# Feed-forward entries of a two-layer model: gate multiplied into the sigmoid ahead, high parts written by ScalarE from the transposes, a first group of five tiles

## The chip, the core and the metric

The kernel runs on one core of a Trainium2 chip. The metric is the device time of one launch in microseconds (us), lower is better. On the core TensorE (PE in the profile) multiplies matrices, VectorE (DVE), ScalarE (ACT) and GpSimd (POOL) work on tiles, and SyncE (SP) issues most transfers. PSUM, where TensorE writes its results, is used as 8 banks of 128 rows by 512 float32 columns. Everything is float32 at the kernel's edges.

## What is computed

A model of two layers, 512 rows of 1024 features. Each layer has a mixer and a feed-forward, each behind an RMS norm that is modulated by a condition vector, and each added to x through a gate vector:

```python
for i in range(DEPTH):                       # DEPTH = 2
    sh_m, sc_m, g_m, sh_f, sc_f, g_f = split(silu(c) @ ada_w[i] + ada_b[i], 6)
    h = rms_norm(x, norm_mix[i]) * (1.0 + sc_m) + sh_m
    y = dsa_attention(h, ...) if i % 2 == 0 else s5_mixer(h, ...)
    x = x + g_m * y
    h = rms_norm(x, norm_ffn[i]) * (1.0 + sc_f) + sh_f
    x = x + g_f * conv_ffn(h, ...)           # up 1024 -> 5632, conv, silu(gate)*val, down to 1024
# the end of s5_mixer:  ga, gb = split(gelu(y) @ w_glu);  return ga * sigmoid(gb)
```

## The kernel before, in words

x lies in SBUF as four blocks of 128 rows (b0 to b3). A float32 product is made of three products of numbers that are split into a high and a low part: high by high, high by low, low by high (`mm3`). So each operand is split once: a high part, rounded to the format `fp32r`, and a low part, the operand minus its high part. Weights arrive by SP's transfers as `raw` tiles; ScalarE casts them to `wh`, VectorE subtracts to `wl`.

All work is written as Python tasks that yield their operations. A planner (`Sched`) picks the next operation by its own costs and writes the instructions of each engine in that order, so the order of a queue is fixed when the kernel is built, and an engine never overtakes. Every operation is recorded at line 310. Where the planner sees a gap of more than 1.6 us ahead on TensorE, it fills it with products whose result nobody uses (`warm`, line 759). Operations that may run on either of two engines (`Alt`) are placed by the planner.

Both feed-forwards are entered through `norm_block` (line 798), once per block of rows. For block b: `norm_rows` squares the rows on ScalarE (`jk`, with the sum in `ss`), VectorE makes `rs_v`, GpSimd raises it to the power -1/2 (`rs_r`), VectorE scales the rows to `xn`. Then for each half of the features (hf 0 and 1, called b1h0 and so on below) TensorE transposes four squares of 128 into one PSUM bank (`nt`), ScalarE applies the modulation to the four (`ht`, in SBUF), VectorE casts the 512 columns to the high part of `H` and subtracts to its low part.

The up-projection in `ffn` (line 1197 on) has 44 weight tiles of 128 columns per layer. A tile is 24 products of 512 columns (8 features blocks by 3). The first group of tiles is made in two parts: part 0 multiplies the columns of blocks b0 and b1 (24 products of 256 columns for each tile), part 1 those of b2 and b3. Part 0 can so begin when `H` of b0 and b1 is written. A tile of the group occupies one PSUM bank from part 0 to the end of part 1.

The feed-forward of layer 1 (FFN1 below) follows the GLU of the mixer: `b_post` takes the sigmoid of the gb products (`sg`), `a_post` multiplies by the ga products (VectorE, `sg<-acc,sg`), by the gate vector (GpSimd, `sg<-sg,gate`), and adds to x (VectorE). These last products (`acc`) end block by block, b0 to b3, 24 products apart; each block then goes to `norm_block`. The feed-forward of layer 0 (FFN0) follows the output projection of the attention in the same way.

Of the kernel before, what the change touches and what calls it, by code (L numbers as in the profile page):

```python
# [14 lines left out]
AF = mybir.ActivationFunctionType  # L15
ALU = mybir.AluOpType
# [3 lines left out]
P = 128  # L20
# [3 lines left out]
KT = 8  # L24
# [147 lines left out]
class Sched:  # L172
# [13 lines left out]
    def spawn(self, gen, prio):  # L186
        t = Task()
        self.n += 1
        t.gen, t.prio, t.ops, t.cond, t.n, t.ready, t.name, t.alts = gen, prio, None, None, self.n, 0.0, gen.__name__, ()
        self.tasks.append(t)  # L190
        self.advance(t)
# [211 lines left out]
def tile_kernel(ctx: ExitStack, tc, t, out):  # L403
    nc = tc.nc
    Z = Sched()
    V, S, G, PE, SP = (Engine(k, e) for k, e in (
        ("V", nc.vector), ("S", nc.scalar), ("G", nc.gpsimd), ("PE", nc.tensor), ("SP", nc.sync)))
# [15 lines left out]
    tmp = Res(Z, tpool, "tmp", TMPS, 512)  # L423
    bank = Res(Z, psum, "bank", 8, 512)
    state = {"side": 0, "side_max": 3, "units": 0, "done": 0}
    flags = set()
    spawn = Z.spawn
# [4 lines left out]
    def need(banks=0, tmps=0, quads=0):  # L432
        return lambda: (state["side"] + banks <= state["side_max"] and bank.free() >= banks
                        and tmp.free() >= tmps and quad.free() >= quads)

    def sbank(name):
        state["side"] += 1
        return bank.get(name)

    def sput(*b):  # L440
        state["side"] -= len(b)
        bank.put(*b)
# [18 lines left out]
    acol = const.tile([P, 4, KT], F32)  # L461
# [93 lines left out]
    gates = {}  # L555
# [242 lines left out]
    def norm_block(b, ni, sh, H, key):  # L798
        xn = yield from norm_rows(b)
        for hf in range(2):  # L800
            yield need(banks=1, tmps=1)
            pt = sbank("nt")
            ht = tmp.get("ht", [P, 4, P])
            yield [PE.transpose(pt[:, j * P:(j + 1) * P], xn[:, (4 * hf + j) * P:(4 * hf + j + 1) * P], ident)
                   for j in range(4)]
            bs = slice(b * P, (b + 1) * P)
            for j in range(4):
                k = 4 * hf + j
                yield S.activation(ht[:, j], pt[:, j * P:(j + 1) * P], AF.Identity, scale=acol[:, ni, k:k + 1],
                                   bias=sh[:, k:k + 1])  # L810
            sput(pt)
            ks = slice(4 * hf, 4 * hf + 4)
            yield V.tensor_copy(H[:, ks, 0, bs], ht)
            yield V.tensor_sub(H[:, ks, 1, bs], ht, H[:, ks, 0, bs])
            tmp.put(ht)
            flags.add((key, hf, b))
        quad.put(xn)
        flags.add((key, b))
# [351 lines left out]
    def ffn(layer, Hs, then, last, hready, mid=None):  # L1170
        yield has("conv")
        A = {}
        vals = {}

        def up_post(m, ps):
            yield need(tmps=1)
            cv = tmp.get("cv")
            w = cw[:, layer, m]
            yield S.activation(cv, ps, AF.Identity, scale=w[:, 2:3], bias=cb[:, layer, m:m + 1])
            yield V.scalar_tensor_tensor(cv[:, 1:], ps[:, :L - 1], w[:, 1:2], cv[:, 1:], op0=ALU.mult, op1=ALU.add)  # L1180
            yield V.scalar_tensor_tensor(cv[:, 2:], ps[:, :L - 2], w[:, 0:1], cv[:, 2:], op0=ALU.mult, op1=ALU.add)
            bank.put(ps)
            if m % 2 == 0:
                vals[m // 2] = cv
                return
            yield S.activation(cv, cv, AF.Silu)
            yield lambda: m // 2 in vals
            yield V.tensor_mul(cv, cv, vals[m // 2])
            tmp.put(vals[m // 2])
            yield lambda: quad.free() >= 1  # L1190
            a = quad.get("a", [P, 2, L], F32R)
            yield S.copy(a[:, 0], cv)
            yield V.tensor_sub(a[:, 1], cv, a[:, 0])
            tmp.put(cv)
            A[m // 2] = a

        def up(m, group, parts):

            ws_ = []
            ps = [None] * group  # L1200
            n = L // parts
            for pt in range(parts):
                for g in range(group):
                    yield lambda: hready((pt + 1) * n)
                    if pt == 0:
                        ws_.append((yield from WS.get()))
                        yield lambda: bank.free() > 0
                        ps[g] = bank.get("up")
                    else:
                        WS.hold = WS.stop = len(plan) if layer else glu0  # L1210
                    wh, wl = ws_[g]
                    o = ps[g][:, pt * n:(pt + 1) * n]
                    for k in range(KT):
                        ws = slice(k * P, (k + 1) * P)
                        h0, h1 = Hs[:, k, 0, pt * n:(pt + 1) * n], Hs[:, k, 1, pt * n:(pt + 1) * n]
                        yield [PE.matmul(o, wh[:, ws], h0, start=(k == 0), stop=False),
                               PE.matmul(o, wh[:, ws], h1, start=False, stop=False),
                               PE.matmul(o, wl[:, ws], h0, start=False, stop=(k == KT - 1))]
                    if pt == parts - 1:
                        quad.put(wh, wl)  # L1220
                        spawn(up_post(m + g, ps[g]), 2)

        for half in range(2):
            i = 0
            while i < 2 * HT:
                g = 4 if half == 0 and i == 0 else 1
                yield from up(2 * HT * half + i, g, 2 if g > 1 else 1)
                i += g
                flags.add(("up", layer, half))
            if half == 1 and mid:  # L1230
                mid()
            k0 = half * HT
            lh = lambda k, b: A[k0 + k][:, 0, b * P:(b + 1) * P]
            ll = lambda k, b: A[k0 + k][:, 1, b * P:(b + 1) * P]
            for ch in range(2):
                fin = then if half and ch else None
                if last and half == 1:
                    def fin(b, ch=ch):
                        yield DM(out[0, b * P:(b + 1) * P, ch * 512:(ch + 1) * 512], x[:, b, ch * 512:(ch + 1) * 512])
                tl = 7 if half and ch and not last else 3  # L1240
                yield from gemm(HT, 512, lh, ll, resid(layer, 5, ch, fin, half and not ch and not last, pre_ssm), tail=tl,
                                ready=lambda k: k0 + k in A,
                                mid=(lambda: quad.put(*[A[k0 + k] for k in range(HT - tl)])) if ch else None)
            quad.put(*[A[k0 + k] for k in range(HT - tl, HT)])
# [578 lines left out]

    sg = {}

    def b_post(b, ps):
        yield need(tmps=1)
        sg[b] = tmp.get("sg")
        yield S.activation(sg[b], ps, AF.Sigmoid)
        bank.put(ps)  # L1830

    def a_post(ch, then):
        def post(b, ps):
            yield lambda: b in sg and (1, 2) in gates
            s_ = sg.pop(b)
            yield V.tensor_mul(s_, ps, s_)
            bank.put(ps)
            yield G.tensor_mul(s_, s_, gates[1, 2][:, ch * 512:(ch + 1) * 512])
            xs = x[:, b, ch * 512:(ch + 1) * 512]
            yield V.tensor_add(xs, xs, s_)  # L1840
            tmp.put(s_)
            if ch:
                yield from then(b)
            else:
                yield from first_half(b)
        return post


    def main():
        yield has("consts")  # L1850
        H = new_H()
# [81 lines left out]
        for b0 in (0, 2):  # L1933
            acc = {}
            for k in range(KT):
                yield lambda: ("g", k // 2) in flags
                if k // 2 == len(tiles):
                    tiles.append((yield from WS.get()))
                w, s_ = tiles[k // 2], k % 2 * 512
                for b in (b0, b0 + 1):  # L1940
                    if b not in acc:
                        yield lambda: bank.free() > 0
                        acc[b] = bank.get("acc")
                    yield mm3(acc[b], gh[0](k, b), gh[1](k, b), w[0][:, s_:s_ + 512], w[1][:, s_:s_ + 512], k == 0, k == KT - 1)
                    if k == KT - 1:
                        spawn(b_post(b, acc[b]), 2)
            state["side_max"] = 4
        quad.put(*[v for w in tiles for v in w])
        state["side_max"] = 3
        yield from gemm(KT, 512, gh[0], gh[1], a_post(0, None), tail=4)  # L1950
        yield from gemm(KT, 512, gh[0], gh[1], b_post, tail=4)
        H1 = new_H()
        yield from gemm(KT, 512, gh[0], gh[1], a_post(1, to_ffn(1, H1)), tail=8)
        quad.put(*[v for q in range(4) for v in HG[q]], gates[1, 2])
# [113 lines left out]
```

## Time and profile before

| what | value |
|---|---|
| median of 3 runs (lowest, highest) | 1284.19 us (1284.01, 1284.42) |
| the profiled execution: its own time | 1281.76 us |
| its span in the trace | 1280.0 us |
| TensorE busy | 1256.0 us, 98% of the span |
| mean granted TensorE clock | 0.997 |
| VectorE, ScalarE, GpSimd busy | 845.5, 519.0, 321.0 us |

The span is the time from the first to the last instruction of the profiled execution; 1.76 us of its own time lie outside of it. That execution is 2.43 us shorter than the median of the runs.

### The profile page before, as it was taken

What the parts mean: (1) busy time and instruction counts of PE and PEld (TensorE: products, weight loads), DVE (VectorE), ACT (ScalarE), POOL (GpSimd) and SP (SyncE); (2) the same over time, 40 slices, a digit from 0 to 9 for tenths busy, and PEclk for the clock granted to TensorE, in tenths of its full rate; (3) what the DMA queues carried; (4) which work ended last, traced back from release to release, by engine and by line L of the source; (5) the groups of instructions that cost most, each with busy time, mean ns of one, the idle gap of its engine ahead of it and who ended that gap; (6) DMA issues with size and microseconds to landing.
All of it is one profiled execution on the core that took longest, in us unless ns stands there. A gap on an engine that the chain in (4) does not pass through costs nothing. (4 is left out here: it accounts for less than half of the span.)

```text
span 1280.0 us, 19538 instructions
## 1 busy us (share of the span) xinstructions
PE 1256.0 (98%) x7314; PEld 993.3 (78%) x7314; DVE 845.5 (66%) x1600; ACT 519.0 (41%) x1124; POOL 321.0 (25%) x525
## 2 busy tenths in 40 slices
PE   7999999999999999999999999999999999999998
PEld 6766577666877678888888887788987888888887
DVE  6688697788677777768775468633787643666632
ACT  4345555556544344234443222423544432244420
POOL 0234446832144256343310302211200001000010
PEclk9999999999999999999999999999999999999999
DMA  9948522101377763445444289322443323322221
GB/s 375 367 161 315 180 82 72 45 34 67 130 291 244 241 234 115 144 173 153 147 127 171 91 183 404 138 100 81 165 133 139 99 91 124 109 76 80 80 88 62
DMA packets 76471, 195.59 MB, mean 153 GB/s; under 512 B 15053, under 2 KB 25805, under 8 KB 76377
## 3 DMA queue, kind: packets, MB, share of 16 engines
q1 hardware_dynamic: 72808, 191.43, 43.4%
q10 hardware_dynamic: 3568, 2.92, 0.8%
q8 instruction: 57, 0.93, 0.3%
q14 instruction: 38, 0.30, 0.1%
HBM read 172.01 MB, written 20.21 MB: 150 GB/s over the span
## 5 line engine op out<-in xcount | busy, mean ns | idle before, releaser
L310 PE MATMUL up<-H,wh 128*128 128x512 f32 (+1 forms) x1536 | 444.7, 374 | 0.0
L310 PEld LDWEIGHTS up<-H,wh 128*128 128x128 f32 x1536 | 277.8, 188 | 61.6 <-issue 12.1
L310 PE MATMUL up<-H,wl 128*128 128x512 f32 (+1 forms) x768 | 285.5, 372 | 0.0
L310 DVE TENSOR_TENSOR wl<-raw,wh 128x1024 fp32r<-128x1024 f32 (+1 forms) x192 | 234.8, 1230 | 61.4 <-ACT wh L310 52.8
L310 PE MATMUL acc<-wh,H 128*128 128x512 f32 (+3 forms) x752 | 241.5, 388 | 1.5 <-ACT H L310 1.4
L310 ACT CAST wh<-raw 128x1024 fp32r<-128x1024 f32 (+1 forms) x192 | 192.5, 1015 | 106.8 <-DMA raw<-in_w_down_dram 41.8
L310 PE MATMUL acc<-wh,a 128*128 128x512 f32 x704 | 219.0, 390 | 0.0
L310 DVE SCALAR_TENSOR_TENSOR cv<-up,sm_b,cv 128x511 f32<-128x511 f32 (+1 forms) x176 | 131.6, 748 | 90.0 <-ACT cv L310 87.0
L310 PEld LDWEIGHTS acc<-wh,H 128*128 128x128 f32 x752 | 138.8, 188 | 46.6 <-issue 20.2
L310 PEld LDWEIGHTS up<-H,wl 128*128 128x128 f32 x768 | 144.6, 188 | 25.3
L310 PEld LDWEIGHTS acc<-wh,a 128*128 128x128 f32 x704 | 132.2, 188 | 27.6 <-issue 0.4
L310 ACT ACTIVATE cv<-up,sm_b 128x512 f32<-128x512 f32 x88 | 68.6, 780 | 197.9 <-PE up L310 180.7
L310 PE MATMUL acc<-wl,H 128*128 128x512 f32 (+3 forms) x376 | 141.4, 376 | 0.0
L310 PE MATMUL acc<-wl,a 128*128 128x512 f32 x352 | 137.0, 389 | 0.0
L310 POOL TENSOR_TENSOR x<-x,rt 128x512 f32<-128x512 f32 x20 | 31.5, 1578 | 416.0 <-DVE rt L310 407.9
L310 DVE TENSOR_TENSOR rt<-acc,gate 128x512 f32<-128x512 f32 x40 | 27.5, 689 | 101.0 <-PE acc L310 101.0
L310 PEld LDWEIGHTS acc<-wl,H 128*128 128x128 f32 x376 | 70.8, 188 | 9.9
L310 PEld LDWEIGHTS acc<-wl,a 128*128 128x128 f32 x352 | 66.1, 188 | 13.6
L310 POOL TENSOR_TENSOR rs_r<-rs_v,nhalf 128x1 f32<-128x1 f32 (+1 forms) x32 | 36.5, 1145 | 99.5 <-DVE rs_v L310 99.4
L310 ACT ACTIVATE cv<-cv 128x512 f32<-128x512 f32 x44 | 27.8, 632 | 68.5 <-DVE cv L310 66.5
L310 POOL TENSOR_TENSOR rm<-rm,rn 128x256 f32<-128x256 f32 (+3 forms) x46 | 37.2, 838 | 62.7 <-DVE rn L310 54.9
L310 PE MATMUL ada<-raw,cond_r 128*32 128x512 f32 (+1 forms) x544 | 49.3, 451 | 2.7 <-ACT xT L310 1.4
(268 smaller groups left out, 1517.4 us busy)
## 6 DMA issues: line engine op xcount, KB each, us to landing
raw<-in_ada_w_dram SPq DMA_DIRECT2D x96, 512.0 KB, 6.4
raw<-in_w_up_dram SPq DMA_DIRECT2D x88, 512.0 KB, 4.1
raw<-in_w_down_dram SPq DMA_DIRECT2D x40, 512.0 KB, 3.5
raw<-in_w_qkv_dram SPq DMA_DIRECT2D x24, 512.0 KB, 6.5
raw<-in_w_glu_dram SPq DMA_DIRECT2D x16, 512.0 KB, 9.3
k_d<-zq SPq DMA_DIRECT2D x8, 512.0 KB, 6.1
raw<-in_w_out_dram SPq DMA_DIRECT2D x8, 512.0 KB, 3.9
p_d<-p SPq DMA_DIRECT2D x16, 256.0 KB, 2.4
```

The lines of the kernel that those rows point to most:

```text
L310: op.fn(*op.a, **op.k)
```

## The change

Four edits. In `norm_block` ScalarE now writes the high part of `H` straight from the transposes in PSUM, and VectorE makes `ht` from the same transposes; the cast of `ht` on VectorE is gone. The first group of up tiles has five tiles in place of four. The gate vector is multiplied into the sigmoid `sg` ahead, on GpSimd or VectorE, and no longer behind the ga products. `b_post` takes the half of the features as an argument for that.

```diff
 # norm_block
             for j in range(4):
                 k = 4 * hf + j
-                yield S.activation(ht[:, j], pt[:, j * P:(j + 1) * P], AF.Identity, scale=acol[:, ni, k:k + 1],
+                yield S.activation(H[:, k, 0, bs], pt[:, j * P:(j + 1) * P], AF.Identity, scale=acol[:, ni, k:k + 1],
                                    bias=sh[:, k:k + 1])
+                yield V.tensor_scalar(ht[:, j], pt[:, j * P:(j + 1) * P], acol[:, ni, k:k + 1], sh[:, k:k + 1],
+                                      op0=ALU.mult, op1=ALU.add)
             sput(pt)
             ks = slice(4 * hf, 4 * hf + 4)
-            yield V.tensor_copy(H[:, ks, 0, bs], ht)
             yield V.tensor_sub(H[:, ks, 1, bs], ht, H[:, ks, 0, bs])
 # ffn
-                g = 4 if half == 0 and i == 0 else 1
+                g = 5 if half == 0 and i == 0 else 1
 # the GLU
-    def b_post(b, ps):
-        yield need(tmps=1)
-        sg[b] = tmp.get("sg")
-        yield S.activation(sg[b], ps, AF.Sigmoid)
-        bank.put(ps)
+    def b_post(ch):
+        def post(b, ps):
+            yield need(tmps=1)
+            s_ = tmp.get("sg")
+            yield S.activation(s_, ps, AF.Sigmoid)
+            bank.put(ps)
+
+            yield lambda: (1, 2) in gates
+            yield Alt(*[E.tensor_mul(s_, s_, gates[1, 2][:, ch * 512:(ch + 1) * 512]) for E in (G, V)])
+            sg[b] = s_
+        return post
     def a_post(ch, then):
         def post(b, ps):
-            yield lambda: b in sg and (1, 2) in gates
+            yield lambda: b in sg
             s_ = sg.pop(b)
             yield V.tensor_mul(s_, ps, s_)
             bank.put(ps)
-            yield G.tensor_mul(s_, s_, gates[1, 2][:, ch * 512:(ch + 1) * 512])
             xs = x[:, b, ch * 512:(ch + 1) * 512]
             yield V.tensor_add(xs, xs, s_)
```

How the instructions stand on three engines at the entry of FFN1 follows; a name before `<-` is what is written, those behind it are read, and `waits` lists the engines or queues whose semaphores the instruction waits for. Of the eight gate multiplies three stand on VectorE now and five on GpSimd, all ahead of the ga products.

ScalarE, at the end of the GLU, before: the squares of b0 (first row), then the two halves of b0 with the squares of b1 between them.

```order
L310 ACTIVATE jk,ss<-x 128x512 [waits DVE_49]
L310 ACTIVATE ht<-nt,mods,acol 128x128 [waits PE_49,Activation_49]
L310 ACTIVATE ht<-nt,mods,acol 128x128 x3
L310 ACTIVATE jk,ss<-x 128x512 [waits DVE_49]
L310 ACTIVATE ht<-nt,mods,acol 128x128 [waits PE_49,Activation_49]
L310 ACTIVATE ht<-nt,mods,acol 128x128 x3
```

The same place of ScalarE with the change:

```order
L310 ACTIVATE jk,ss<-x 128x512 [waits DVE_49]
L310 ACTIVATE H<-nt,mods,acol 128x128 [waits PE_49]
L310 ACTIVATE H<-nt,mods,acol 128x128 [waits DVE_49] x3
L310 ACTIVATE jk,ss<-x 128x512
L310 ACTIVATE H<-nt,mods,acol 128x128 [waits PE_49]
L310 ACTIVATE H<-nt,mods,acol 128x128 [waits DVE_49] x3
```

Before, the second to fourth activation of a half waited for nothing; now each of them waits for VectorE.

VectorE at the same place, before: the ga product and x of b0, `xn` of b0, x of b1, the two halves of b0 with `rs_v` and `xn` of b1 between them.

```order
L310 TENSOR_TENSOR sg<-acc,sg 128x512 [waits PE_49]
L310 TENSOR_SCALAR xn<-x,rs_r 128x1024 [waits Pool_49]
L310 TENSOR_TENSOR x<-x,sg 128x512 [waits Pool_49]
L310 CAST H<-ht 128x4x128 [waits Activation_49]
L310 TENSOR_TENSOR H<-ht,H 128x4x128 [waits DVE_49]
L310 TENSOR_SCALAR rs_v<-ss,e_9136 128x1 [waits Activation_49]
L310 TENSOR_SCALAR xn<-x,rs_r 128x1024 [waits Pool_49]
```

VectorE with the change, from `xn` of b0 to the low part of b0's second half:

```order
L310 TENSOR_SCALAR xn<-x,rs_r 128x1024 [waits Pool_49]
L310 TENSOR_TENSOR sg<-acc,sg 128x512 [waits PE_49]
L310 TENSOR_SCALAR ht<-nt,acol,mods 128x128 [waits Activation_49]
L310 TENSOR_TENSOR x<-x,sg 128x512 [waits DVE_49]
L310 TENSOR_SCALAR ht<-nt,acol,mods 128x128 [waits Activation_49] x3
L310 TENSOR_TENSOR H<-ht,H 128x4x128 [waits DVE_49]
L310 TENSOR_SCALAR rs_v<-ss,e_9166 128x1 [waits Activation_49]
L310 TENSOR_SCALAR ht<-nt,acol,mods 128x128 [waits Activation_49] x2
L310 TENSOR_SCALAR xn<-x,rs_r 128x1024 [waits Pool_49]
L310 TENSOR_SCALAR ht<-nt,acol,mods 128x128 [waits Activation_49] x2
L310 TENSOR_TENSOR H<-ht,H 128x4x128 [waits DVE_49]
```

Four `ht` instructions stand where one cast stood, each of them waits for ScalarE, and `xn` of b1 stands between the second and the third `ht` of b0's second half.

TensorE, the last rows of the GLU and the first of the up-projection, before:

```order
L310 MATMUL acc<-wl,H 128x512
L310 MATMUL acc<-wh,H 128x512
L310 MATMUL nt<-sm_a,xn 128x128 x4
L759 MATMUL warm<-sm_a 128x128 x17
L310 MATMUL up<-H,wh 128x256 x2
L310 MATMUL up<-H,wl 128x256
```

TensorE with the change:

```order
L310 MATMUL acc<-wl,H 128x512
L310 MATMUL acc<-wh,H 128x512
L310 MATMUL nt<-sm_a,xn 128x128 x4
L310 MATMUL acc<-wh,H 128x512
L310 MATMUL acc<-wl,H 128x512
L310 MATMUL acc<-wh,H 128x512
L310 MATMUL up<-H,wh 128x256 x2
L310 MATMUL up<-H,wl 128x256
```

The `warm` products are gone, and the transposes have moved: in the change those of b0h0, b0h1, b1h0, b1h1 and b2h0 stand 48, 36, 27, 15 and 3 products ahead of the up-projection (before, b0h0 to b1h1 stood 39, 27, 18 and 0 products ahead of it), and b2h1, b3h0 and b3h1 stand behind 42, 69 and 99 of the 120 products of part 0 (before, b2's and b3's four stood behind 30, 39, 51 and 63 of 96). At the entry of FFN0 five `warm` and at that of FFN1 seventeen are gone, for which the trace has ten and 34 records; the other `warm` of the program stay. There too b2h0 now stands three products ahead of the up-projection, and b2h1 and b3h0 48 and 69 products into part 0.

## Rows read from the trace of the kernel before

**Rows 1.** The page, parts 1 (busy us, share, instructions) and 2 (granted clock).

```profile
PE 1256.0 (98%) x7314; PEld 993.3 (78%) x7314; DVE 845.5 (66%) x1600; ACT 519.0 (41%) x1124; POOL 321.0 (25%) x525
PEclk9999999999999999999999999999999999999999
```

**Rows 2.** The chain that ended last, from FFN1's entry: start us, us, what.

```profile
907.98 0.44 PE nt L310 x4
908.42 3.80 PE warm L759 x34
912.22 3.59 PE up L310 x30
...
921.50 42.70 PE up L310 x249
...
1036.14 59.84 PE acc L310 x264
```

**Rows 3.** Timeline, FFN1's entry: start us, us, engine, operation, [idle before, releaser].

```profile
890.26 0.69 DVE L310 TENSOR_TENSOR sg<-acc,sg 128x512 f32<-128x512 f32 x1 [1.51 <-PE acc L310]
...
891.10 1.28 POOL L310 TENSOR_TENSOR sg<-sg,gate 128x512 f32<-128x512 f32 x1 [25.53 <-DVE sg L310]
...
892.41 0.69 DVE L310 TENSOR_TENSOR x<-x,sg 128x512 f32<-128x512 f32 x1 [1.46 <-POOL sg L310]
...
893.14 0.63 ACT L310 ACTIVATE jk<-x 128x512 bf16<-128x512 f32 x1 [5.84 <-DVE x L310]
...
894.19 0.55 POOL L310 TENSOR_TENSOR rs_r<-rs_v,nhalf 128x1 f32<-128x1 f32 x1 [1.81 <-DVE rs_v L310]
...
896.31 0.74 DVE L310 TENSOR_SCALAR xn<-x,rs_r 128x1024 f32<-128x1024 f32 x1
...
897.55 0.60 PE L310 MATMUL nt<-sm_a,xn 128*128 128x128 f32 x4
...
898.25 1.50 ACT L310 ACTIVATE ht<-nt,mods,acol 128x128 f32<-128x128 f32 x4 [4.38 <-PE nt L310]
...
900.25 0.69 DVE L310 TENSOR_TENSOR H<-ht,H 128x512 fp32r<-128x512 f32 x1
```

**Rows 4.** The tile `ht`: min, median and max ns of its instructions.

```profile
L310 ACT ACTIVATE ht<-nt,mods,acol x64: 447/457/464, 335.5 to 923.6; 128x128 f32<-128x128 f32 x64
```

**Rows 5.** VectorE's groups by form: busy us, mean ns, idle before (`pt` is in PSUM).

```profile
L310 DVE COPY pT<-pt 128x128 f32<-128x128 f32 x9 | 2.5, 285 | 1.5 <-PE pt L310 1.3
...
L310 DVE TENSOR_SCALAR ct<-c_in 128x128 f32<-128x128 f32 x4 | 1.4, 348 | 0.0
...
L310 DVE TENSOR_SCALAR c_in<-c_in 128x128 f32<-128x128 f32 x4 | 0.9, 220 | 0.0
```

**Rows 6.** Timeline, two engines that read one PSUM bank (`pv`).

```profile
764.19 0.42 DVE L310 COPY U<-pv 128x256 f32<-128x256 f32 x1 [0.98 <-PE pv L310]
764.64 0.37 ACT L310 COPY U<-pv 128x256 f32<-128x256 f32 x1 [1.89 <-DVE U L310]
```

**Rows 7.** Timeline, the split of one weight tile.

```profile
908.63 1.22 DVE L310 TENSOR_TENSOR wl<-raw,wh 128x1024 fp32r<-128x1024 f32 x1
...
909.90 1.05 ACT L310 CAST wh<-raw 128x1024 fp32r<-128x1024 f32 x1
```

**Rows 8.** Timeline of TensorE, FFN0's entry.

```profile
340.60 0.60 PE L310 MATMUL nt<-sm_a,xn 128*128 128x128 f32 x4
...
348.14 0.40 PE L310 MATMUL up<-H,wh 128*128 128x256 f32 x2
...
363.31 1.28 PE L759 MATMUL warm<-sm_a 128*128 128x128 f32 x10
```

**Rows 9.** Windows: length, busy us (instructions) of each engine, granted clock, DMA share, GB/s.

```profile
0.00:16.00 16.00, 10.22 (x112) 8.41 (x113) 8.53 (x33) 8.31 (x18) 2.71 (x8) 1.00 0.90 346
750.00:762.00 12.00, 9.46 (x84) 9.16 (x82) 5.81 (x13) 3.27 (x10) 0.80 (x5) 1.00 1.04 192
762.00:770.00 8.00, 8.00 (x96) 7.82 (x96) 4.89 (x12) 2.03 (x3) 0.00 (x0) 0.57 1.04 404
```

More of the change, by code (lines that the diff above doesn't have):

```diff
@@ L1945, in main @@
                     if k == KT - 1:
-                        spawn(b_post(b, acc[b]), 2)
+                        spawn(b_post(0)(b, acc[b]), 2)
             state["side_max"] = 4
@@ L1950, in main @@
         yield from gemm(KT, 512, gh[0], gh[1], a_post(0, None), tail=4)
-        yield from gemm(KT, 512, gh[0], gh[1], b_post, tail=4)
+        yield from gemm(KT, 512, gh[0], gh[1], b_post(1), tail=4)
         H1 = new_H()
```

## The prediction

> **What bounds the kernel now.** I read the page first: TensorE is busy 98% of the span at a granted clock of nine tenths or more in every slice [rows 1]. So a change pays only through what TensorE executes, or through time in which it waits. The chain of waits says the same at the places that the change touches: from FFN1's entry on every piece is TensorE's, piece behind piece. Two prices come from it. A product of 512 columns costs 59.84 / 264 = 0.227 us, one of 256 columns 3.59 / 30 = 0.12 us, and four transposes 0.44 us [rows 2]. And there is one piece that does no work: 3.80 us of `warm`, between the last transposes and the first up product. There TensorE has nothing to do until `H` of b1 is written. FFN0's entry has a smaller such piece, 1.28 us, within part 0 [rows 8]. Behind 921.50 the 249 up products (129 of 256 columns and 120 of 512, 15.5 + 27.2 = 42.7 us) run without a wait [rows 2]. So before, each entry costs TensorE only its `warm`: what feeds it is just fast enough.
>
> The timeline shows how that feeding runs, for one block. From the end of x of b0 to `rs_r` it takes 892.41 + 0.69 to 894.19, so 1.1 us, and `rs_r` and `xn` take 0.55 and 0.74. For one half, the first transpose starts at 897.55, the four activations at 898.25 (0.70 later) and last 1.50, and the low part ends at 900.94: 2.7 us from the first activation to the end of `H` [rows 3]. Neither ScalarE nor VectorE holds the other up within the four squares.
>
> **What the change removes and adds on TensorE.** Gone are the two `warm` pieces, 3.80 + 1.28 = 5.1 us. A fifth tile in two parts is 48 products of 0.12 in place of 24 of 0.227: 0.32 us more in each layer, 0.64 in all [rows 2]. If all else stays hidden, that is a gain of 4.4 us. [...]
>
> **The gate edit.** Behind the ga product GpSimd's multiply goes, 1.28 us here with its hops from 890.95 to 892.41 = 1.46 us, so x of a block is complete 1.4 us sooner [rows 3]. The eight multiplies ahead stand where VectorE and ScalarE wait for products; I cost them at nothing, for TensorE works on the GLU meanwhile and nothing reads `sg` until the ga products end. Were that cover gone it would be a VectorE row of 0.69 for each of three.
>
> **The price of a pair.** This is the step that decides. ScalarE's write to `H` and VectorE's `ht` read one bank, and each now waits for the other: the four squares go ScalarE, VectorE, ScalarE, VectorE. The trace shows that a second reader of a bank starts only behind the first: 764.19 + 0.42, then 764.64, a hop of 0.03 us [rows 6]. An activation of a square is 0.457 us [rows 4]. `ht` on VectorE from PSUM is not in the trace. The nearest row in size and source is the copy of a 128x128 square from PSUM, 0.285; the nearest in operation, both in SBUF, are 0.220 and 0.348 [rows 5]. I take 0.285, for its source is the same, and keep the other two as bounds. A pair is then 0.457 + 0.03 + 0.285 + 0.04 = 0.81 us (0.745 to 0.875), four of them 3.2, and with the low part 0.69 a half takes 3.9 us where it took 2.7. [...]
>
> Worse than the 1.2 us: both queues are in order, so whatever stands between two `ht` (x, `xn`, the 1.22 us subtraction of a weight tile, [rows 7]) now stops ScalarE too, and ScalarE's squares and its 1.05 us casts stop VectorE. For one block eight pairs take 6.5 us, two low parts 1.4, and `xn`, the ga product and x 2.1, some of it beside an activation: about 9 us. TensorE gives one block every 24 x 0.227 + 2 x 0.44 = 6.3 us. So it will wait, more with each block.
>
> **FFN1, followed through the new order** (times on the axis of before; order from the three engines' rows). The acc products end at 907.98; without three interleaved transposes of 0.44 and with b0h0's 48 products ahead of their end, those transposes start at 895.8, and the first activation at 896.5 or so. Pair 1 ends at 897.4; VectorE then adds x of b1 (to 898.1), so pair 2 ends at 898.4, pairs 3 and 4 at 899.2 and 900.0, the low part at 900.7. The squares of b1 stand behind the fourth activation on ScalarE and end at 900.5, `rs_r` at 901.5. The first pairs of b0h1 run from 900.5 to 902.1, and only then `xn` of b1, to 902.9. TensorE reaches b1h0's transposes at 901.4: **1.5 us of wait**. The rest of b0h1 ends at 904.7, b1h0 with the ga product and x of b2 in between at 908.9, the squares of b2 at 909.1, three pairs of b1h1 at 911.5, `xn` of b2 at 912.3. TensorE is at b2h0's transposes at 909.1: **3.2 us**. Three products later the up-projection starts, about 913.4, where it started at 912.22 behind its `warm`. In part 0 b2's pairs share VectorE and ScalarE with two or three weight tiles (1.22 and 1.05 each), x of b3 ends at 919.6, its squares stand behind a cast and end at 920.4, `xn` of b3 at 924.3. TensorE comes to b3h0 69 products (8.3 us) and one set of transposes into part 0, 922.0: **2.3 us**. Part 1 starts at 931.3 and wants b3h1 after 12 products, at 932.7; that half's four pairs and two weight subtractions end at 934.2: **1.5 us**. Together 8.5 us.
>
> **FFN0 likewise.** b1h0's transposes stand where they stood, 340.60, and `xn` of b1 comes behind six pairs, the squares and a low part at 341.8: **1.2 us**. b2h0's come 24 products later, at 348.1 with that wait, `xn` of b2 at 351.2: **3.0**, so the up-projection starts about 352.4, not 348.14 [rows 8]. b3h0: two weight casts and subtractions and two chunks of transfers on ScalarE's queue stand among b2's pairs; `xn` of b3 at 365.1, TensorE there at 362.1: **3.0**. Its last half ends about when part 1 asks. Together 7.2 us.
>
> **Sum.** -5.1 + 0.64 + 8.5 + 7.2 = +11.3 us on the 1281.76 us of the profiled execution: 1293.0. The runs' median lies 2.43 above it: **1295.4 us**. Pairs at 0.745 or 0.875 instead of 0.81, about 26 in each layer on this path: 3.4 us less or more, 1292.0 to 1298.8.
>
> **Rivals.**
> *Half the waits.* My chain goes by medians and lets no activation start before its transposes are all done; if the waits are half as long (7.9 us), the time is 1287.6; at a third, 1285.0. For it: VectorE's other work fits partly beside activations. Against: the strict alternation leaves little beside.
> *The change does what it says (the other side).* The pairs stay ahead of TensorE, because x comes 1.4 us sooner and b0's transposes stand nine products earlier, and `warm` is replaced by work: -4.4 us, 1279.8. It decides at a block of 6.3 us on VectorE and ScalarE: then no lead is lost. Against: the eight pairs alone take 6.5. Break-even is at waits of 4.4 us in all.
> [...]
>
> **Numbers.** 0.2% of the time, 2.6 us, is about what a measurement of this kernel can tell from no change. Forecast, 1291 to 1299: 0.58. Clock or dearer pairs, above that: 0.12. A third to half of the waits: 0.18, of which 0.07 within 0.2% of before. Hidden: 0.12, of which 0.08 faster and 0.04 within. So faster 0.08, same 0.11, slower 0.81. The range runs from 1285 to 1300: it leaves out the hidden case and the dearest part of the clock's.
>
> **What would show it.** In the trace after: `ht` from `nt` on VectorE at about 0.285 us, activations of squares 0.8 us apart where they were 0.35; no `warm` at the two entries; TensorE waiting for `xn` at b1h0, b2h0 and b3h0, most at b2h0; the up-projection of FFN1 starting about as late as before in spite of 3.8 us less `warm`; a granted clock as before. I am wrong if activations and `ht` overlap, if TensorE's waits at the entries stay under 5 us in all, or if something outside of the two entries moves by more than 1 us.

## Result: 1297.6 us, 1.2% slower

The changed kernel took 1297.59 us (median of 4 runs, 1295.40 to 1298.89) against 1284.10 before (4 runs, 1283.67 to 1284.42). The ratio is 1.0116, 95% interval 1.0102 to 1.0130. The profiled execution took 1298.14 us with a span of 1296.4.

The page's parts 1 and 2 of the changed kernel, against [rows 1]:

```profile
PE 1261.0 (97%) x7318; PEld 997.2 (77%) x7318; DVE 862.6 (67%) x1631; ACT 525.0 (40%) x1124; POOL 326.7 (25%) x542
PEclk9999999999999999999999989999899999999999
```

TensorE is busy 5 us longer in a span that is 16.4 us longer: most of the loss is idle time. Its waits by what they waited for (total us, times, longest), the two largest of the rows that the kernel before does not have:

```profile
PE nt L310 <- DVE xn L310: 10.9, 6, 3.2
...
PE up L310 <- DVE H L310: 1.9, 1, 1.9
```

Their places in the timeline of TensorE, FFN0 first (the bracket is the idle time before the row):

```profile
343.69 0.63 PE L310 MATMUL nt<-sm_a,xn 128*128 128x128 f32 x4 [1.36 <-DVE xn L310]
...
353.40 0.66 PE L310 MATMUL nt<-sm_a,xn 128*128 128x128 f32 x4 [3.13 <-DVE xn L310]
...
367.45 0.66 PE L310 MATMUL nt<-sm_a,xn 128*128 128x128 f32 x4 [1.31 <-DVE xn L310]
...
911.87 0.66 PE L310 MATMUL nt<-sm_a,xn 128*128 128x128 f32 x4 [1.27 <-DVE xn L310]
...
921.66 1.11 PE L310 MATMUL nt<-sm_a,xn 128*128 128x128 f32 x4 [3.19 <-DVE xn L310]
...
935.01 0.66 PE L310 MATMUL nt<-sm_a,xn 128*128 128x128 f32 x4 [0.66 <-DVE xn L310]
...
945.70 0.38 PE L310 MATMUL up<-H,wh 128*128 128x256 f32 x1 [1.94 <-DVE H L310]
```

In each entry these are the transposes of b1h0, b2h0 and b3h0, in that order; the last row is part 1 of FFN1, which waits for the low part of b3h1. Together 12.9 us. The `warm` of [rows 2] and [rows 8] is gone.

The chain that ended last, from FFN1's entry on (start us, us, what), is no longer TensorE's alone:

```profile
904.85 0.45 PE nt L310 x4
905.32 0.47 ACT H L310
905.82 0.41 DVE ht L310
906.23 0.60 DVE x L310
906.83 0.35 DVE ht L310
907.20 0.47 ACT H L310
907.69 0.42 DVE ht L310
...
921.66 1.11 PE nt L310 x4
922.78 1.28 PE acc L310 x3
924.06 6.62 PE up L310 x42
...
1052.52 59.84 PE acc L310 x264
```

For 17 us it runs through the pairs: ScalarE, VectorE, ScalarE, VectorE, with x of the next block between two of them. The up-projection starts at 924.06, 11.8 us later than in [rows 2]; the down-projection at 1052.52, 16.4 later. The price of a pair stands in the timeline of the two engines:

```profile
906.14 0.68 DVE L310 TENSOR_TENSOR x<-x,sg 128x512 f32<-128x512 f32 x1
906.26 0.46 ACT L310 ACTIVATE H<-nt,mods,acol 128x128 fp32r<-128x128 f32 x1 [0.48 <-DVE ht L310]
906.75 0.41 DVE L310 TENSOR_SCALAR ht<-nt,acol,mods 128x128 f32<-128x128 f32 x1
907.20 0.46 ACT L310 ACTIVATE H<-nt,mods,acol 128x128 fp32r<-128x128 f32 x1 [0.48 <-DVE ht L310]
```

From one activation to the next 0.94 us (906.26 to 907.20), of which ScalarE idles 0.48. Before, four activations took 1.50 in one piece [rows 3]. `ht` takes 0.41 us. The tile `ht` (min, median and max ns; then idle time of its engine before it, and who waited for it) sums it up:

```profile
L310 DVE TENSOR_SCALAR ht<-nt,acol,mods x64: 398/410/413, 337.6 to 944.5; 128x128 f32<-128x128 f32 x64
...
  ACT H L310: 18.8, 39
...
  ACT H L310: 28.8, 43
```

VectorE idled 18.8 us for ScalarE's `H` (39 times), and ScalarE 28.8 us for VectorE's `ht` (43 times).

And one thing beside the waits: the windows around b2h0's waits (length, busy us, then the granted clock third from the right):

```profile
354.00:358.00 4.00, 4.00 (x20) 3.77 (x19) 3.07 (x9) 1.01 (x3) 2.80 (x11) 0.57 0.23 58
...
922.00:928.00 6.00, 6.00 (x29) 5.71 (x27) 3.51 (x6) 2.68 (x5) 0.00 (x0) 0.54 0.31 115
928.00:932.00 4.00, 4.00 (x36) 4.00 (x35) 4.00 (x7) 2.97 (x6) 0.00 (x0) 1.00 0.41 116
```

Behind each of the two waits of 3.1 and 3.2 us TensorE worked for some microseconds at about half of its clock: 0.57 and 0.54 on the mean of these windows, 0.50 in each single microsecond from 355 to 357 and from 922 to 927 us, and 1.00 from 358 to 366 and from 928 to 935 us. By the windows' clocks, 0.43 x 4 + 0.46 x 6 = 4.5 us of full speed were lost there (an estimate; how much of it the kernel's time shows is taken up below). [rows 9] show such a stretch in the kernel before, 8 us at 0.57.

### The profile page after: what moved, and what is told of

It is laid out like the page before. It is cut to its first block, busy times and chain, and to the rows that moved or that the text cites. A ratio compares the mean times of both kernels' runs of the same rounds, so it can differ in the third digit from the quotient of the medians.

```text
span 1296.4 us, 19552 instructions
## 1 busy us (share of the span) xinstructions
PE 1261.0 (97%) x7318; PEld 997.2 (77%) x7318; DVE 862.6 (67%) x1631; ACT 525.0 (40%) x1124; POOL 326.7 (25%) x542
## 5 line engine op out<-in xcount | busy, mean ns | idle before, releaser
L310 PE MATMUL up<-H,wh 128*128 128x512 f32 (+1 forms) x1568 | 449.5, 372 | 1.9 <-DVE H L310 1.9
L310 PEld LDWEIGHTS up<-H,wh 128*128 128x128 f32 x1568 | 284.1, 190 | 62.6 <-issue 12.1
L310 PE MATMUL up<-H,wl 128*128 128x512 f32 (+1 forms) x784 | 289.4, 369 | 0.0
L310 PEld LDWEIGHTS up<-H,wl 128*128 128x128 f32 x784 | 149.1, 190 | 24.9
L310 POOL TENSOR_TENSOR C<-u,u 128x144 f32<-128x144 f32 x48 | 33.4, 711 | 104.3 <-DVE u L310 74.9
```

The source lines that it names most:

```text
L310: op.fn(*op.a, **op.k)
```

## The experiments

The theory: ScalarE and VectorE read one bank in strict alternation, a half takes too long, and TensorE waits for `xn` and `H`. The rivals: the five tiles (banks held, products split), the gate edit (work moved to VectorE), VectorE's greater work in itself, and the lower clock rather than the waits. Medians of different groups of runs come from different chips (the kernel before took 1283.12, 1281.94 and 1284.66 us on the three of this section), so the ratio to the kernel before, run on the same chip, is what counts.

**Undo the norm block.** The changed kernel with `norm_block` of before:

```diff
-                yield S.activation(H[:, k, 0, bs], pt[:, j * P:(j + 1) * P], ...)
-                yield V.tensor_scalar(ht[:, j], pt[:, j * P:(j + 1) * P], ...)
+                yield S.activation(ht[:, j], pt[:, j * P:(j + 1) * P], ...)
+            yield V.tensor_copy(H[:, ks, 0, bs], ht)
```

> The changed kernel with the norm block of before (four activations to ht, one cast, one subtraction); the gate ahead and the five tiles stay. If the alternation of ScalarE and VectorE on one bank is the cause, the waits for xn at the two entries (10.9 us in the changed kernel), the 1.9 us wait for the low part and the stretches at the lower clock go, and what is left is the sum without waits, -5.1 + 0.64: 1279 to 1282 us. If the five tiles or the gate edit are the cause, it stays at 1293 us or more.

Measured 1277.50 us against 1283.12, ratio 0.9953 (0.9939 to 0.9968): not only no loss, but faster than before, and below the expected band. The chain at FFN1's entry:

```profile
908.90 0.44 PE nt L310 x4
909.34 1.39 PE acc L310 x6
910.73 4.68 PE up L310 x39
...
922.46 37.65 PE up L310 x238
```

It is TensorE's alone again, with no `warm` and no wait: the gate edit and the five tiles do what the sum without waits said. The whole loss goes with the norm block's edit.

**Each edit alone on the kernel before.** First the norm block, as in the change's diff:

> The kernel before with the new norm block alone. If the alternation is the cause: 1294 to 1302 us, with waits for xn of 10 us or more in all. If it needs the other edits beside it: within 3 us of before.

1305.64 us, ratio 1.0168 (1.0151 to 1.0185), above the expected band: worse than the whole change. Its waits by what they waited for:

```profile
PE nt L310 <- DVE xn L310: 10.7, 5, 3.1
...
PE up L310 <- DVE H L310: 4.4, 4, 2.2
```

15.1 us, and beside them `warm` products that the planner put where TensorE then had a wait as well, in FFN1's part 0:

```profile
941.17 4.47 PE L759 MATMUL warm<-sm_a 128*128 128x128 f32 x24
...
945.91 1.50 PE L759 MATMUL warm<-sm_a 128*128 128x128 f32 x12
```

The gate edit alone:

> The kernel before with the gate edit alone. Its order has no warm at FFN1's entry any more, so if the feeding keeps up it gains that, 1280 to 1282 us. If the gate edit's work on VectorE and GpSimd is what holds TensorE up, 1287 us or more.

1279.96 us, ratio 0.9970 (0.9960 to 0.9979), at the lower edge of what was expected: it takes the `warm` at FFN1's entry away, since x of a block is complete sooner and the transposes move ahead.

The five tiles alone (`g = 5`):

> The kernel before with the five tiles alone. Its order loses the warm at FFN0's entry (1.28 us) and keeps that at FFN1's; the split costs 0.64: 1283 to 1285 us. If five banks held by the first group starve the side work: 1287 us or more.

1284.21 us, ratio 1.0000 (0.9988 to 1.0011), as expected: no change that the runs can tell, and no harm. The two rivals among the edits fall.

**The same instructions without the alternation.** First, one handover of the bank for a half in place of seven:

```diff
             for j in range(4):
                 yield S.activation(H[:, k, 0, bs], pt[:, j * P:(j + 1) * P], ...)
+            for j in range(4):
                 yield V.tensor_scalar(ht[:, j], pt[:, j * P:(j + 1) * P], ...)
```

> The changed kernel with all four activations of a half ahead of the four VectorE instructions: one handover of the bank in a half in place of seven, the same instructions otherwise. If the alternation is the cause: ScalarE is free after 1.5 us, a half takes about 1.5 + 4 x 0.41 + 0.69 = 3.8 us with VectorE 2.3 us busy, so a block takes VectorE about 6.7 us against 6.3 of TensorE: waits of 2 to 8 us in all, 1280 to 1288 us. If VectorE's 0.41 us for each square is the cause by itself: 1293 us or more.

1281.63 us, ratio 0.9989 (0.9978 to 1.0001). A half in its timeline:

```profile
902.97 1.50 ACT L310 ACTIVATE H<-nt,mods,acol 128x128 fp32r<-128x128 f32 x4 [1.07 <-PE nt L310]
904.88 1.36 DVE L310 TENSOR_SCALAR ht<-nt,acol,mods 128x128 f32<-128x128 f32 x4
...
906.27 0.69 DVE L310 TENSOR_TENSOR H<-ht,H 128x512 fp32r<-128x512 f32 x1
```

Four activations take 1.50 us again, so 0.35 from one to the next, and four `ht` behind one another 1.36, so 0.32. In a row each instruction thus overlaps its neighbour by about 0.1 us (0.46 and 0.41 us long, 0.35 and 0.32 apart), which the alternation gives up, together with a hop of 0.03 to 0.04 at each change of engine. A half takes 3.6 us from its first activation to the end of its low part for b0h0 (899.79 to 903.42), where the first one of the changed kernel takes 4.45 (905.32 to 909.77). And the engines no longer stop each other: over the whole program VectorE idles 2.1 us for `H` in place of 18.8, and ScalarE never for `ht`. This reordering alone takes the ratio from 1.0116 to 0.9989.

Second, two banks for a half, two squares in each; ScalarE begins with one bank, VectorE with the other:

```diff
-            pt = sbank("nt")
+            pts = [sbank("nt"), sbank("nt2")]
+            sq = lambda j: pts[j // 2][:, (j % 2) * P:(j % 2 + 1) * P]
...
+                i = (j + 2) % 4
-                yield V.tensor_scalar(ht[:, j], pt[:, j * P:(j + 1) * P], ...)
+                yield V.tensor_scalar(ht[:, i], sq(i), ...)
```

> The changed kernel with the transposes of a half in two banks, two squares in each: ScalarE begins with one, VectorE with the other, and they change once. The same eight instructions for a half. If the shared bank is the cause: a half takes about 2 x 0.41 + 0.05 + 2 x 0.41 + 0.69 = 2.4 us, nearly all waits go, 1277 to 1282 us. If the count or the price of VectorE's instructions is the cause: 1290 us or more.

1281.40 us, ratio 0.9995 (0.9986 to 1.0004). Its timeline at FFN1's entry:

```profile
897.52 0.81 ACT L310 ACTIVATE H<-nt,mods,acol 128x128 fp32r<-128x128 f32 x2 [3.49 <-PE nt L310]
897.91 1.05 DVE L310 TENSOR_SCALAR ht<-nt,acol,mods 128x128 f32<-128x128 f32 x3
898.67 0.81 ACT L310 ACTIVATE H<-nt,mods,acol 128x128 fp32r<-128x128 f32 x2 [0.34 <-DVE ht L310]
```

The two engines read transposes at once, from two banks: ScalarE from 897.52 to 898.33, VectorE from 897.91 on. The instructions are the changed kernel's, eight for a half, so neither their number nor VectorE's greater work is the cause: taking turns on one bank, square by square, is. A bank that is handed over once does little harm, as the run ahead of this one shows (1.0 us of waits for `xn`, where the changed kernel has 10.9). The planner laid both versions anew, but their transposes of b0h0 to b2h0 stand about where the changed kernel's do: 48, 36, 27, 12 and 3 products ahead of FFN1's up-projection with one handover, 48, 39, 30 and 18 ahead and 3 behind its start with two banks. So it is not that TensorE asks for its blocks later. No run here lets the two engines read one bank at once (in the changed kernel each of a half's instructions behind its first waits for the other engine), so what that would do to the time is not shown.

**The clock.** Twelve products without use ahead of b2's first transposes, at both entries:

```diff
+            if b == 2 and hf == 0:
+                yield [PE.matmul(pt[:, :P], ident, ident, start=True, stop=True) for _ in range(12)]
             yield [PE.transpose(...) for j in range(4)]
```

> The changed kernel with twelve products without use on TensorE ahead of the transposes of b2's first half, at both entries: they lie in the time in which TensorE waits 3.1 us for xn, 24 records or about 2.7 us. If the lower clock behind those waits is a cost of its own (6 us at 0.50 and 3 us at 0.53 to 0.62 in the changed kernel, so about 4.5 us in all): 1292 to 1294 us and a granted clock of 1.00 at the entries. If the waits alone make the time: 1297 us or a little more.

1294.12 us, ratio 1.0102 (1.0086 to 1.0117). The kernel before took 1281.94 on this chip, so the band in microseconds says little, and by the ratio the gain on 1.0116 lies within the intervals. Windows of it:

```profile
922.00:928.00 6.00, 5.63 (x48) 5.43 (x47) 5.35 (x10) 3.97 (x7) 1.46 (x1) 1.00 0.47 155
936.00:940.00 4.00, 1.32 (x12) 1.12 (x10) 2.91 (x6) 1.38 (x3) 0.00 (x0) 1.00 0.39 117
940.00:944.00 4.00, 3.82 (x19) 3.82 (x20) 0.44 (x2) 0.78 (x1) 0.00 (x0) 0.57 0.08 29
```

The clock stays at 1.00 behind b2h0's transposes, but a wait of 2.9 us later on, for a low part, now has the stretch at 0.57 behind it. Nor is the fill free: its products take 2.84 us at each entry and a wait of 1.14 and 1.17 is left, at each place 0.8 more than the wait alone was. So I ran it beside the changed kernel, the undone norm block and the two banks on one chip, all four unchanged.

> The changed kernel again, on one chip with the three that follow, so that they are compared directly: 1.010 to 1.013 of before.

> The fill kernel again beside the changed one. The fill took the lower clock at b2's transposes away (about 4.7 us in the changed kernel's windows) and got one such stretch later, 4 us at 0.57 or 1.7 us. If the clock is a cost of its own: 2 to 3.5 us below the changed kernel. If not: within 1 us of it.

The changed kernel 1298.24 us, ratio 1.0108 (1.0090 to 1.0127); the fill 1296.77, ratio 1.0096 (1.0077 to 1.0114). The difference of 1.5 us lies between the two conditions of the expectation and within the intervals. In this execution of the changed kernel, too, the clock was lower for a shorter time: 0.98 on the mean of 890 to 960 us, against 0.95 in the first. The time of that stage did not follow (table below): less was lost to the clock behind b2h0, but TensorE then waited 1.62 us at b3h0 in place of 0.66:

```profile
932.72 0.66 PE L310 MATMUL nt<-sm_a,xn 128*128 128x128 f32 x4 [1.62 <-DVE xn L310]
```

There the lower clock made TensorE late for a block that was not ready anyway. FFN0's stage is 1.4 us shorter with the fill than in this execution of the changed kernel, and 2.8 shorter than in the first. So what the clock costs by itself is some 1 to 3 us (an estimate from these stages, with what the fill costs in it), and it is not the cause of the loss.

> The old norm block with the gate ahead and five tiles again: 0.994 to 0.997 of before, the best of the kernels.

1278.94 us, ratio 0.9952 (0.9937 to 0.9967): repeated. This is the version to take, 0.5% faster than before.

> The two banks again. Its waits at the entries are about 1 us in all, so by them it should lie within 1.5 us of the old norm block; its first ratio, 0.9995, was 5 us above that. If the two differ by their work: 0.998 to 1.000. If it was the start of the runs that differed: 0.995 to 0.997.

1282.77 us, ratio 0.9987 (0.9977 to 0.9998): the first condition of the expectation held, so the two banks are by some 4 us slower than the undone norm block, though their profiles show under 1 us of waits at the entries and spans that are less than 1 us apart (1280.0 and 1279.2). The two profiles are not typical of their runs: that of the undone norm block is the slowest of its six (1281.03), that of the two banks the second fastest of its twelve (1281.81).

**The same runs, by stages.** TensorE's order is the same in all kernels here up to the last `po` product of the attention, and that product starts anywhere between 320.7 and 325.2 us. A comparison of whole spans carries this scatter; stages behind it do not. FFN0's stage runs here from the start of the last `po` product to that of the first `pu` product (in layer 1's mixer), FFN1's from the start of the last `pg` product (ahead of the GLU) to the end of the span. The rows of the three tiles (min, median and max ns; first and last start), of the kernel before and of the changed one:

```profile
L310 PE MATMUL po<-pT,vt x320: 272/273/324, 145.8 to 320.7; 128*64 128x128 f32 x160
L310 PE MATMUL pu<-sm_a,XU x32: 273/275/322, 755.2 to 758.7; 96*128 96x96 f32 x32
L310 PE MATMUL pg<-sm_a,gy x32: 270/272/328, 783.7 to 825.2; 128*128 128x128 f32 x32
...
L310 PE MATMUL po<-pT,vt x320: 272/273/324, 147.3 to 322.2; 128*64 128x128 f32 x160
L310 PE MATMUL pu<-sm_a,XU x32: 273/286/364, 765.1 to 769.2; 96*128 96x96 f32 x32
L310 PE MATMUL pg<-sm_a,gy x32: 270/272/328, 792.6 to 834.5; 128*128 128x128 f32 x32
```

Worked out from such rows and the spans:

| kernel (profiles) | FFN0's stage, us | FFN1's stage, us |
|---|---|---|
| before | 434.5 | 454.8 |
| changed (two) | 442.9, 441.5 | 461.9, 461.8 |
| fill (two) | 440.2, 440.1 | 462.1, 462.1 |
| norm block undone (two) | 432.9, 432.9 | 451.4, 451.3 |
| norm block alone | 443.8 | 468.1 |
| gate edit alone | 434.6 | 451.5 |
| five tiles alone | 432.9 | 455.0 |
| one handover | 434.2 | 452.7 |
| two banks (two) | 434.7, 434.8 | 452.0, 452.0 |

Two executions of one kernel agree within 0.1 us here, but for FFN0 of the changed one. The gate edit takes 3.3 us off FFN1, the five tiles 1.6 off FFN0 (which their runs could not tell), and the norm block puts 8.6 to 10 and 10.5 on. Of the 4 us between the two banks and the undone norm block 2.5 show: 1.8 to 1.9 in FFN0's stage, where the `ada` products (18.09 us busy against 17.05) make 1.0 of it, and 0.6 to 0.7 in FFN1's. The rest is open.

## Why the prediction was right, and where its terms were off

**What bounds, and the pair as the step that decides: shown.** Without the norm block's edit there are no waits; with the same instructions on two banks, or with one handover, nearly none (0.4 and 1.0 us for `xn`).

**-5.1 us of `warm` and +0.64 for the split: right as a sum.** Gate and five tiles together gave a ratio of 0.9953, so 4.1 to 7.8 us less by its interval; -4.4 lies in it, near its smaller end; by the stages it is -1.6 and -3.4, where the sum has -0.96 and -3.48. That was my rival on the other side, and it holds once the norm block is undone. I had put the loss of the `warm` down to the whole change; the single runs divide it: the gate edit takes that of FFN1 away, the five tiles that of FFN0.

**The price of a pair: too low.** `ht` is 0.41 us, above both bounds (0.220 and 0.348), so a pair is 0.94, not 0.81. The copy from PSUM, 0.285, was the wrong neighbour. My bounds came from operations that are nearest in size, and none had both PSUM as its source and two scalars for each row; the range should have been wider to the top.

**The waits: the places right, the sum too large.** For b1h0 I had 1.2 and 1.5, for b2h0 3.0 and 3.2: measured 1.36 and 1.27, 3.13 and 3.19. For b3h0 I had 3.0 and 2.3: measured 1.31 and 0.66. For the low part of b3h1 1.5: measured 1.94. Together 15.7 against 12.9, so the rival of half the waits falls too. By my own rule, 0.13 us more for each of 52 pairs would have put 6.8 us on top. It did not, as far as the rows show, because my chain gave every instruction its whole duration: `ht` starts at 906.75 though the row of x ahead of it ends at 906.82, and four `ht` in a row take 0.32 each. So two errors offset each other: `xn` of b1 ends 7.1 us behind the start of b0h0's transposes in FFN1, as in my chain. No run separates the two.

At b3h0 the chain on VectorE and ScalarE came when I had said: `xn` of b3 ends 12.4 and 10.9 us behind the start of the up-projection, forecast 12.7 and 10.9. TensorE was late instead: it was ready for these transposes 11.2 and 10.3 us behind that start, forecast 9.7 and 8.6, for the stretches at a clock of 0.57 and 0.54 lie in between. The rows of `xn` of b3, FFN0's first:

```profile
366.65 0.74 DVE L310 TENSOR_SCALAR xn<-x,rs_r 128x1024 f32<-128x1024 f32 x1
...
934.21 0.74 DVE L310 TENSOR_SCALAR xn<-x,rs_r 128x1024 f32<-128x1024 f32 x1
```

**The clock: a cost that my sum left out.** I gave the clock and dearer pairs a chance of 0.12 together. The windows show 4.5 us of lost clock in the profiled execution, and 3.3 us less waiting than forecast at the two b3h0: these are mostly one thing, for what the clock took there the wait gave back. My sum left out the one and had the other too large. Partly luck remains: the pair's price and the overlap that I denied it offset each other, and the shift of 2.43 us from profile to median did not repeat (the profiled execution is 0.55 us above the median now). As a difference, I forecast +11.3; the medians differ by 13.5, the spans by 16.4.

**The rest.** -4.4 + 12.9 + 4.5 = 13.0 us, of 16.4 us in the spans. By stages the 16.4 are 1.5 ahead of the last `po`, 8.4 in FFN0's stage, -0.6 between the stages and 7.1 in FFN1's. The first 1.5 is no effect of the change: in this execution the clock was 0.72 from 18 to 24 us, where the order of TensorE is the same as before, and 1.00 in the profile before. In FFN0's stage 1.8 us are left over its terms; 0.8 of them are two waits of 0.42 (for a weight's low part and at an `ada` product), and the second profile of the same kernel is 1.4 us shorter there. In FFN1's 0.8 are left; these are open. My sign "a granted clock as before" did not come true either: also away from the entries it was lower, 0.63 from 770 to 780 us and 0.86 from 800 to 812, but the stretch between the two stages took no longer for it.

## What to carry to other kernels

Two engines that took turns on one PSUM bank, instruction by instruction, ran in lockstep here: each step cost both durations and both hops (0.94 us, where four in a row cost 0.35 and 0.32 each), and what stood ahead of a turn in VectorE's queue stopped ScalarE as well (it idled 1.13 us ahead of 914.15 us, where a low part of 0.69 us stood ahead of `ht`, and 0.48 us ahead of the next activations). Before moving a step to "run beside" another, look whether they read one bank; if so give each engine its own bank or let one finish before the other starts (ratios of 0.9995 and 0.9989 here, against 1.0116), and check the whole half against the time that TensorE leaves for it. And undo edits of a bundle one by one: here two of them held a gain of 0.5% that the third hid under a loss of 1.6%. Where single runs scatter by more than an edit is worth, compare stages that begin behind the scatter.

## What I had not expected of the hardware

A `tensor_scalar` of a 128x128 square from PSUM with two per-row scalars takes 0.41 us alone and 0.32 in a row of four, where a copy of the same square takes 0.285. In the changed kernel's profile the waits of 3.1 and 3.2 us were followed by 4 and 6 us at a clock of 0.57 and 0.54, and the waits of 1.3 us were not (1.00 from 344 to 350, from 368 to 374 and from 912 to 918 us); in a second execution of the same kernel less was lost at FFN1 (0.98 on the mean of 890 to 960 us, against 0.95), and its stage took the same time (461.8 us, against 461.9). And the first 90 us differ from execution to execution with the clock: `kt`, the same instruction behind the same order of TensorE in every kernel here, starts at 87.1 to 87.8 us in the three profiles whose granted clock from 18 to 30 us was 1.00, at 88.6 to 90.1 in the six with 0.86, and at 90.2 to 91.5 in the four with 0.72.
